# Running the last two units of an output product, and the first two of the next, token tile by token tile

## The chip, the cores and the metric

One core of a Trainium2 chip runs the whole kernel. The metric is the device time of that core in microseconds (us), and the time of a kernel is the median over its runs.

## The reference

A trunk of two layers works on 256 tokens of width 2048, in float32. Each layer is a token mixer, a cross attention into 256 fixed memory tokens (4 heads of 128), and an MLP with squared ReLU (2048 to 8192 and back). Layer 0's mixer is an mLSTM, layer 1's a gated DeltaNet with 32 value heads of 128 and a gate `z`. Every sub-layer is wrapped in two norms:

```python
for i in range(DEPTH):
    g = norm_g[i]
    h = rms_norm(x, g[0])
    mix = mlstm_mixer(h, ...) if i == 0 else gdn_mixer(h, ...)
    x = x + rms_norm(mix, g[1])
    h = rms_norm(x, g[2])
    x = x + rms_norm(mem_cross_attn(h, k_m, v_m, w_xq[i], w_xo[i]), g[3])
    h = rms_norm(x, g[4])
    x = x + rms_norm(sq_relu_mlp(h, w_up[i], w_down[i]), g[5])
```

and the end of the gated DeltaNet is `o = rms_norm(o, norm_g) * silu(z)`, then `o @ w_out`.

## The kernel before

**Precision and weights.** A float32 product is made of three matmuls on numbers split into a high part and a rest: high x high, high x rest, rest x high. Weights stream from memory in units of 4 blocks of 128 rows by 512 columns, each unit as two halves (`raw`, 512 KB each, 4 buffers). For each half ACT casts the high part (L89) and DVE subtracts to get the rest (L90); there are two buffers of each. `ws.add` lists the order of all units once; `ws.take` hands out the next one and starts the one after. `extra_unit` puts the first unit of the next product into tiles of the hidden units that are free by then (names `xw`, lines L85 and L86).

**Products.** `h` holds the sub-layer's input feature-major (features on the 128 partitions, the 256 tokens along the row, high part then rest), in 16 blocks of 128 features.
- `prod_feat` gives a feature-major result: weights are the stationary operand, 512 and 256 columns wide per step (L318, L319) or, narrow, three of 256 (L322 to L324). `fresh` makes the first four blocks narrow. `prod_tall` is the narrow form for one block of columns at a time (L337 to L339).
- `prod_tok` gives a token-major result (tokens on the partitions), in chunks of 512 columns: the input's token tile `t` (0 or 1, 128 tokens each) is stationary and 512 weight columns move (L384 to L386). For each unit it runs t=0, 12 matmuls, then t=1, 12 more.

**From one product to the next.** The output products m_out, xo, down and g_out are token-major, since the norm behind them is over a token's features. `Post.take` gets each chunk as it is done: sum of squares on ACT (`Rms.add`, L232), product with the norm's gain on DVE. With the last chunk (`ch == 3`) of a token tile it makes the reciprocal root `rpost` (`rstd`: L485 reduction, L487 or L489 and L490 root, L491 reciprocal). `advance` then adds the normed result to the residual stream `xk` (`residual`, L496, four chunks by two token tiles), transposes `xk` on PE (`feed`, L214, tiles `ltp`, eight transposes for each chunk), and splits the transposes into the new `h` (ACT L249, then DVE L250, 256 tokens wide). It also sums squares of the new `xk` for the next norm. `behind` fixes the order of some of these against each other. There are five such boundaries: m_out to xq, xo to up (layer 0), down to the gated DeltaNet's first product gq, g_out to xq, xo to up (layer 1). The last `down` has `stagger=True`: its last two units run t=0 of both, then t=1 of both, and each token tile goes to the output as it is done.

**Cross attention.** `xq` runs feature-major, narrow, for three heads, `ev_q` makes the scores and the softmax, and the fourth head's query is a `prod_tall` of its own.

**Gated DeltaNet.** The eight groups of four value heads run one after the other in `core`. A group loads `vt`, `tf`, `tn` and, last, `ab` (1.5 MB, single buffer, issued by the POOL queue), starts with small matmuls `np` (L1156) that need `ab`, and ends with `op` (L1218), the last reader of `ab`, and the transposes `otp` (L1241). Between the groups run the gate products `gz` (96 matmuls each, `gate(g4)`, groups 0 to 3, just ahead of the group's `core`) and, from group 4 on, the output product `g_out`. The gates of groups 4 to 7 are made earlier (`early_z`), kept in memory (`z_d`) and loaded by the POOL queue.

The order of instructions on each engine is fixed when the program is built: a scheduler places them by priority, and gives the DeltaNet's weight splits a higher one (`ws.first = 400`).

Of the kernel before, what the change touches and what calls it, by code (L numbers as in the profile page):

```python
# [14 lines left out]
P = 128  # L15
# [3 lines left out]
UK = 4  # L19
# [94 lines left out]
def trunk(ctx: ExitStack, tc, x, mem, norm_g, mem_norm_g, w_mem_kv, w_xq, w_xo, w_up, w_down,  # L114
# [22 lines left out]
    for l in range(2):  # L137
        if l == 1:
            g_in, g_out = gdn_w_in[0], gdn_w_out[0]
            for c in range(4):  # L140
                ws.add("gq", g_in, 0, D, c * 512, 512, tall=c > 0)
                ws.add("gk", g_in, 0, D, 2048 + c * 512, 512, tall=True)
                if c == 0:
                    ws.add("ab", g_in, 0, D, GDN_QKV + GDN_Z, 64, tall=True)
                ws.add("gz", g_in, 0, D, GDN_QKV + 2048 + c * 512, 512)
            ws.add("gv", g_in, 0, D, 4096, 4096, tall=True)
            ws.add("gz", g_in, 0, D, GDN_QKV, 2048)
            for half in range(2):
                ws.add("g_out", g_out, half * 2048, 2048, 0, D)
# [146 lines left out]
    def prod_feat(key, srcs, n_fb, evac, wide=True, before=None, fresh=False):  # L296


        nk = len(srcs)
        for c0 in range(0, n_fb, 4):  # L300
            nf = min(4, n_fb - c0)
            accs, k = None, 0
            while k < nk:
# [9 lines left out]
                w_ = wide and not (fresh and c0 == 0)  # L313
                for f, j in order:
                    a, kk = accs[f], k + j
                    wh, wl = hi[j][:, f * P : f * P + fw], lo[j][:, f * P : f * P + fw]
                    if w_:
# [8 lines left out]
            for f in range(nf):  # L326
                evac(c0 + f, Bank(accs[f], w_))
# [30 lines left out]
    def prod_tok(key, srcs, n_ch, evac, after=None, post=None, stagger=False, start=None):  # L358
# [3 lines left out]
        for c in range(n_ch):  # L362
            if start:
                start(c)
            accs = [acc(f"{key}{c}_{t}") for t in range(2)]
            k, units = 0, []
            while k < nk:
                final = post is not None and c == n_ch - 1 and k + UK >= nk
                if post is not None and (n_ch - c) * nk - k == 2 * UK:
                    extra_unit(4 if nk == UK else 0)  # L370
                hi, lo, kb, n = ws.take(key, 1 if final else None)
                if final:
                    post.halves = ws.begin()
                units.append((k, hi, lo, kb))
                k += kb
                if stagger and c == n_ch - 1 and k == nk - UK:
                    continue
                for t in range(2):
                    for k0, hi, lo, kb in units:
                        for j in range(kb):  # L380
                            kk = k0 + j
                            sh = srcs[kk][:, t * P : (t + 1) * P]
                            sl = srcs[kk][:, T + t * P : T + (t + 1) * P]
                            PE.matmul(accs[t], sh, hi[j], start=(kk == 0), stop=False)  # L384
                            PE.matmul(accs[t], sh, lo[j], start=False, stop=False)  # L385
                            PE.matmul(accs[t], sl, hi[j], start=False, stop=(kk == nk - 1))  # L386
                if after:
                    after(units[-1][0] // UK)
                units = []
            for t in range(2):  # L390
                evac(c, t, accs[t])
# [46 lines left out]
    class Post:  # L438


        def __init__(self, l, s, bias=None):
            self.l, self.s, self.bias, self.halves, self.g, self.r, self.late = l, s, bias, [], {}, [], []
            self.y = [acts.tile([P, 2, 512], F32, tag=f"y{c}", name=f"y{c}") for c in range(4)]
            self.rms = Rms("post")
# [12 lines left out]
        def take(self, ch, t, a, plus=False):  # L457

            d = self.y[ch][:, t, :]
            if plus:  # L460
                v = self.add(ch, t, a, False)
                a = d
            last = ch == 3 and t == 0 and self.halves
            if last:
                behind(self.rms.add(a, t, ch), self.halves.pop(0)()[0])
            else:
                self.rms.add(a, t, ch)
            if ch == 0 and t == 0:
                S.sqrt(warm, self.rms.ss[:, 0, 0:1])
            if ch == 3:  # L470
                self.r.append(self.rstd(t))
                late = lambda: V.tensor_tensor(d, a, self.g[ch], ALU.mult)
                if t == 0 and not plus:
                    late()
                else:
                    self.late.append(late)
                self.added = v if plus else None
# [5 lines left out]
        def rstd(self, t):  # L483
            r = small.tile([P, 1], F32, tag=f"rpost{t}", name="rpost")
            V.tensor_reduce(r, self.rms.ss[:, t, :], AX.X, ALU.add)  # L485
            if self.bias is None:
                S.activation(r, r, AF.Sqrt, bias=eps_t, scale=1.0 / D)  # L487
            else:
                V.scalar_tensor_tensor(r, r, 1.0 / D, self.bias[:, t : t + 1], ALU.mult, ALU.add)  # L489
                S.sqrt(r, r)  # L490
            V.reciprocal(r, r)  # L491
            return r

# [4 lines left out]
    def advance(post, nxt):  # L498

        rms = Rms("x")  # L500
        h = new_h()
        halves = post.halves
        r0 = post.residual(0, 0)
        if post.added:
            behind(r0, post.added)
        for ch in range(4):
            if ch:
                behind(post.residual(ch, 1), hv)
            else:
                hv = post.residual(0, 1)  # L510
            if ch < 3:
                behind(post.residual(ch + 1, 0), hv)
            ha, hv = feed(xk[ch], ch, h, lambda k: gain(nxt[0], nxt[1], k))
            if ch == 0:
                for late in post.late:
                    behind(late(), hv)
            for t in range(2):
                behind(rms.add(xk[ch][:, t, :], t, ch), ha)
            if ch < 2:
                for half in halves:  # L520
                    a, v = half()
                    behind(a, ha)
                    behind(v, hv)
                halves = ws.begin() if ch == 0 else []
        return h, rms
# [94 lines left out]
    def mlstm(sc, h, rms, before):  # L620
# [119 lines left out]
        return out_proj("m_out", y, 0, 1)  # L740

    def out_proj(key, y, l, s):
        post = Post(l, s)
        prod_tok(key, y, 4, post.take, post=post)
        return post


    def cross(sc, l, h, rms):
# [8 lines left out]
        def scales(c):  # L757
            if c == 3:
# [23 lines left out]
        prod_feat("xq", h, XA_H - 1, ev_q, wide=False, before=scales)  # L782
# [16 lines left out]
        return out_proj("xo", o, l, 3)  # L799
# [22 lines left out]
    def mlp(l, h, rms):  # L822
        post = Post(l, 5)
# [5 lines left out]
        post.bias = mlp_bias(rms)  # L829
        if l == 0:  # L830
            prod_tok("down", u, 4, lambda ch, t, a: post.take(ch, t, a, True), post=post)
            return post

        def last(ch, t, a):
            post.take(ch, t, a, True)
            if ch == 3:
                while post.late:
                    post.late.pop()()
# [5 lines left out]
        prod_tok("down", u, 4, last, stagger=True)  # L844
# [19 lines left out]
    def gdn(g0, h, rms):  # L864
# [8 lines left out]
        z_d = tc.dram_tile([4, P, 2, 512], F32, name="z_d")  # L873
# [36 lines left out]
        with tc.tile_pool(name="gd1", bufs=1) as sc:  # L910
# [126 lines left out]
            def early_z(c):  # L1037
# [6 lines left out]
                prod_tok("gz", h, 1, ev)  # L1044

            for c in range(4):
# [8 lines left out]
                early_z(c)  # L1055
# [64 lines left out]
        with tc.tile_pool(name="gd3", bufs=1) as sc:  # L1120
            post = Post(1, 1)
# [190 lines left out]
```

## Time and profile before

| | us |
|---|---|
| median of 3 runs | 2911.84 |
| the runs | 2912.97, 2911.84, 2908.85 |
| the profiled execution | 2910.57 |
| its span in the profile | 2908.8 |

The span is the time between the first and the last instruction that the profile records; 1.77 us of the execution's own time lie around it. Rows of the profile name an engine (PE is the matrix engine, PEld its load of the stationary operand, DVE the vector engine, ACT the scalar engine, POOL and SP mostly issue transfers), a line of the kernel (L214), the operation, the tiles that it writes and reads, and a count (x192). Of times, "busy" is the sum over instructions and "idle before" the time for which the engine waited, with what ended it. Matmuls are pipelined, so that their recorded lengths overlap. A window row gives the length of a stretch and for each engine the busy time and number of instructions in it, the granted clock of PE as a share of full speed (PEclk), the share of the transfer engines in use and GB/s.

### The profile page before, as it was taken

The page shows a single profiled execution, that of the slowest core. Times are in us where ns is not written, and L with a number is a line of the kernel's source. Part 1 is how long each engine was busy: PE and PEld are TensorE (multiplying, and loading weights), DVE is VectorE, ACT ScalarE, POOL GpSimd, SP SyncE. Part 2 cuts the span into 40 slices and gives each one's busy share as a digit, 9 for nine tenths or more (in the row PEclk, how much of TensorE's full clock was granted, in tenths as well). Part 3 has the DMA queues.
Part 4 walks back from the last instruction along what each step waited for, and adds up shares of the span by engine and source line. Part 5 has one row for each costly group of instructions (what it writes and reads, how often), then busy time and mean ns, then how long its engine had stood idle before and what let it go on. Part 6 is the DMA issues. An engine that isn't in the chain of part 4 may idle for free.

```text
span 2908.8 us, 42441 instructions
## 1 busy us (share of the span) xinstructions
PE 2866.5 (99%) x16683; PEld 2478.6 (85%) x16683; DVE 1756.9 (60%) x2603; ACT 1427.3 (49%) x2127; POOL 142.3 (5%) x295
## 2 busy tenths in 40 slices
PE   8999999999999999999999999999999999999998
PEld 7888888888888888799998997878888888888887
DVE  5554657654545555577776885554576545455565
ACT  6444546644434434467664545444465444344443
POOL 0000000000000000002212112220000000000000
PEclk9999999999999999999999999999999999999999
DMA  7545664555565555658778787664545555655555
GB/s 249 182 146 177 191 204 145 181 191 193 186 197 188 189 189 188 206 160 247 228 219 235 204 222 254 210 228 164 197 158 168 188 190 188 198 185 192 192 187 168
DMA packets 378411, 566.07 MB, mean 195 GB/s; under 512 B 23873, under 2 KB 156738, under 8 KB 375906
## 3 DMA queue, kind: packets, MB, share of 16 engines
q1 hardware_dynamic: 363456, 507.12, 56.0%
q0 software_dynamic: 13184, 54.90, 5.7%
q8 instruction: 131, 2.15, 0.3%
q10 hardware_dynamic: 1570, 1.33, 0.1%
q14 instruction: 70, 0.57, 0.1%
HBM read 535.94 MB, written 27.33 MB: 194 GB/s over the span
## 4 chain that ended last, share of the span: by engine, by line
PE 90%; DVE 4%; DMA 3%; ACT 1%; issue 1%; POOL 0%; DVEq 0%; ACTq 0%; POOLq 0%
PE up L318 15%; PE up L319 8%; PE down L384 8%; PE down L385 8%; PE down L386 8%; PE o L318 2%; PE g_out L386 2%; PE g_out L384 2%; PE g_out L385 2%; DMA raw<-in_gdn_w_in 2%; PE gz L384 2%; PE gz L386 2%; PE gz L385 2%; DVE lo L90 1%; PE gk L337 1%
## 5 line engine op out<-in xcount | busy, mean ns | idle before, releaser
L90 DVE TENSOR_TENSOR lo<-raw,hi 128x1024 fp32r<-128x1024 f32 x938 | 1110.2, 1217 | 895.1 <-ACT hi L89 894.1
L89 ACT CAST hi<-raw 128x1024 fp32r<-128x1024 f32 x938 | 943.4, 1046 | 944.7 <-PE down L386 314.3
L318 PE MATMUL up<-h,hi 128*128 128x512 f32 x1920 | 678.7, 399 | 0.0
L319 PE MATMUL up<-h,lo 128*128 128x256 f32 x1920 | 539.3, 281 | 0.0
L318 PEld LDWEIGHTS up<-h,hi 128*128 128x128 f32 x1920 | 360.8, 188 | 89.9
L385 PE MATMUL down<-lo,u 128*128 128x512 f32 x1024 | 398.5, 389 | 0.0
L384 PE MATMUL down<-hi,u 128*128 128x512 f32 x1024 | 398.4, 389 | 0.0
L386 PE MATMUL down<-hi,u 128*128 128x512 f32 x1024 | 398.3, 389 | 0.0
L319 PEld LDWEIGHTS up<-h,lo 128*128 128x128 f32 x1920 | 362.7, 189 | 0.2
L384 PEld LDWEIGHTS down<-hi,u 128*128 128x128 f32 x1024 | 192.2, 188 | 40.0
L386 PEld LDWEIGHTS down<-hi,u 128*128 128x128 f32 x1024 | 192.2, 188 | 40.0
L385 PEld LDWEIGHTS down<-lo,u 128*128 128x128 f32 x1024 | 192.2, 188 | 39.6
L337 PE MATMUL gv<-h,hi 128*128 128x256 f32 x512 | 147.1, 287 | 3.2 <-ACT hi L89 3.2
L339 PE MATMUL gv<-h,lo 128*128 128x256 f32 x512 | 146.6, 286 | 1.7 <-DVE lo L90 1.7
L338 PE MATMUL gv<-h,hi 128*128 128x256 f32 x512 | 145.9, 285 | 0.0
L384 PE MATMUL gz<-hi,h 128*128 128x512 f32 x256 | 103.7, 405 | 0.0
L337 PEld LDWEIGHTS gv<-h,hi 128*128 128x128 f32 x512 | 99.2, 194 | 3.8 <-ACT hi L89 3.4
L386 PE MATMUL gz<-hi,h 128*128 128x512 f32 x256 | 102.3, 400 | 0.0
L385 PE MATMUL gz<-lo,h 128*128 128x512 f32 x256 | 102.2, 399 | 0.0
L339 PEld LDWEIGHTS gv<-h,lo 128*128 128x128 f32 x512 | 99.2, 194 | 2.4 <-DVE lo L90 2.3
L338 PEld LDWEIGHTS gv<-h,hi 128*128 128x128 f32 x512 | 99.2, 194 | 0.2 <-issue 0.2
L889 DVE SCALAR_TENSOR_TENSOR cv<-pad,cols,cv 128x256 f32<-128x256 f32 x192 | 90.9, 480 | 6.3 <-ACT cv L887 3.8
(438 smaller groups left out, 4688.2 us busy)
## 6 DMA issues: line engine op xcount, KB each, us to landing
raw<-in_w_up SPq DMA_DIRECT2D x256, 512.0 KB, 4.0
raw<-in_w_down SPq DMA_DIRECT2D x256, 512.0 KB, 4.2
raw<-in_gdn_w_in SPq DMA_DIRECT2D x192, 512.0 KB, 5.0
raw<-in_mlstm_w_in SPq DMA_DIRECT2D x96, 512.0 KB, 3.9
raw<-in_gdn_w_out SPq DMA_DIRECT2D x64, 512.0 KB, 4.2
raw<-in_mlstm_w_out SPq DMA_DIRECT2D x32, 512.0 KB, 4.1
at_d<-at POOLq DMA_DIRECT2D x8, 1536.0 KB, 8.2
ab<-at_d POOLq DMA_DIRECT2D x8, 1536.0 KB, 6.9
```

The costliest lines, as they stand in the source:

```text
L89: a = nc.scalar.copy(h_, raw[:, :, :n])
L90: return a, nc.vector.tensor_tensor(l_, raw[:, :, :n], h_, ALU.subtract)
L318: PE.matmul(a[:fw], wh, srcs[kk][:, :], start=(kk == 0), stop=False, skip_group_check=True)
L319: PE.matmul(a[:fw, T:], wl, srcs[kk][:, 0:T], start=False, stop=(kk == nk - 1), skip_group_check=True)
L337: PE.matmul(a[:, 0:T], hi[k], srcs[k][:, 0:T], start=(k == 0), stop=False)
L338: PE.matmul(a[:, 0:T], hi[k], srcs[k][:, T:], start=False, stop=False)
L339: m = PE.matmul(a[:, 0:T], lo[k], srcs[k][:, 0:T], start=False, stop=(k == nk - 1))
L384: PE.matmul(accs[t], sh, hi[j], start=(kk == 0), stop=False)
L385: PE.matmul(accs[t], sh, lo[j], start=False, stop=False)
L386: PE.matmul(accs[t], sl, hi[j], start=False, stop=(kk == nk - 1))
L889: V.scalar_tensor_tensor(c, pad[:, j : j + T], w[j], c, ALU.mult, ALU.add)
```

## The change

1. `prod_tok` takes the last two units of a product that a `Post` follows together: t=0 of both, then t=1 of both (24 matmuls each). It does the same with the first two units of a product that has a `lead`.
2. `rpost` needs fewer steps at the end: `take` sums the first three chunks' squares and adds the bias ahead, with chunk 2 (`pre`). For t=0 the residuals of chunks 0 and 1 follow at once.
3. The transposes of a chunk go by token tile (`half`): four 128 x 128 transposes into one bank, then four 128-wide splits on ACT and four on DVE. For t=0, chunk 0's stand six matmuls before the end of the old product (`ahead`), chunk 1's right after it (`advance`); t=1's of chunks 0 and 1 stand between the parts of the next product's lead (`between`), and chunks 2 and 3 follow whole (`both`).
4. The next product begins token-major with its first two units: xq's three heads (384 wide, transposed back from `qtok`), the first 512 hidden units of `up` (transposed and split from `utok`). Ahead of gq stands a chunk of gz, the one that group 3's gate used to make in `gate(3)`; it is kept in `z_d` and group 3 now loads its gate as groups 4 to 7 do.
5. The last `down`'s `stagger` is now `split`, the same order.

```diff
+            ws.add("gz", g_in, 0, D, GDN_QKV + 1536, 512)
             for c in range(4):
...
-            ws.add("gz", g_in, 0, D, GDN_QKV, 2048)
+            ws.add("gz", g_in, 0, D, GDN_QKV, 1536)
...
+        pairs, i = [], 0
+        while i < len(steps):
+            two = i == 0 and lead or i == len(steps) - 2 and (post or split)
+            pairs.append((i, i + 1) if two else (i,))
+            i += len(pairs[-1])
+        for p_ in pairs:
+            last = p_[-1] == len(steps) - 1
+            if post and last:
+                extra_unit(4 if nk == UK else 0)
+            for i in p_:
+                fetch(i)
             for t in range(2):
-                evac(c, t, accs[t])
+                for i in p_:
+                    if t and i == p_[-1] and last and post:
+                        post.halves = ws.begin()
+                        run(i, t, 0, UK // 2)
+                        post.ahead()
+                        run(i, t, UK // 2)
+                    else:
+                        run(i, t)
+                    if lead and p_[0] == 0:
+                        lead.between(t * 2 + i)
+                    done(i, t)
...
+            if ch == 2:
+                p_ = self.pre[t] = small.tile([P, 1], F32, tag=f"pre{t}", name="pre")
+                V.tensor_reduce(p_, self.rms.ss[:, t, 0:3], AX.X, ALU.add)
+                V.scalar_tensor_tensor(p_, p_, 1.0 / D, self.bias[:, t : t + 1] if self.bias is not None else eps_t,
+                                       ALU.mult, ALU.add)
             if ch == 3:
-                self.r.append(self.rstd(t))
...
+                S.activation(r, self.rms.ss[:, t, 3:4], AF.Sqrt, bias=self.pre[t], scale=1.0 / D)
+                V.reciprocal(r, r)
+                if self.nxt and t == 0:
+                    self.residual(0, 0)
+                    self.residual(1, 0)
+                    self.late()
...
+        def half(self, ch, t):
+            p_ = psum(f"lth{ch}")
+            for i in range(4):
+                PE.transpose(p_[:, i * P : (i + 1) * P], xk[ch][:, t, i * P : (i + 1) * P], ident)
+            for i in range(4):
+                kb = ch * 4 + i
+                if t == 0:
+                    self.h[kb] = acts.tile([P, 2 * T], F32R, tag=f"h{kb}", name=f"h{kb}")
+                g_, d, s_ = gain(*self.nxt, kb), self.h[kb], p_[:, i * P : (i + 1) * P]
+                S.activation(d[:, t * P : (t + 1) * P], s_, AF.Copy, scale=g_)
+                V.scalar_tensor_tensor(d[:, T + t * P : T + (t + 1) * P], s_, g_, d[:, t * P : (t + 1) * P],
+                                       ALU.mult, ALU.subtract)
+        def both(self, ch):
+            for t in range(2):
+                self.residual(ch, t)
...
+            feed(xk[ch], ch, self.h, lambda k: gain(*self.nxt, k))
+        def ahead(self):
+            self.half(0, 0)
+            for half in self.halves:
+                half()
+        def advance(self):
+            self.half(1, 0)
...
+        def between(self, i):
+            if i == 0:
+                self.residual(0, 1)
+                self.half(0, 1)
+            elif i == 1:
+                self.residual(1, 1)
+                self.half(1, 1)
+                self.late()
+            elif i == 2:
+                self.both(2)
+            else:
+                self.both(3)
...
-        prod_feat("xq", h, XA_H - 1, ev_q, wide=False, before=scales)
+        prod_tok("xq", h, 1, lambda c, t, a: (V.tensor_copy, S.copy)[t](qtok[t], a), after=scales, lead=lead)
+        for f in range(XA_H - 1):
+            p_ = psum("xqt")
+            for t in range(2):
+                PE.transpose(p_[:, t * P : (t + 1) * P], qtok[t][:, f * P : (f + 1) * P], ident)
+            ev_q(f, Bank(p_, False))
...
+            if c == 0:
+                prod_tok("up", h, 1, first, lead=lead)
             u = new_u()
-            prod_feat("up", h, KB, relu2(u), fresh=c == 0)
+            if c == 0:
+                feed(d, 0, u, lambda k: None)
+            prod_feat("up", h, KB, relu2(u), f0=0 if c else 4)
...
+            early_z(0, lead)
...
-                early_z(c)
+                early_z(c + 1)
...
             def gate(g4):
                 zs = sc.tile([P, 2, 512], F32, tag="zs", bufs=2, name="zs")
+                if g4 > 2:
+                    nc.gpsimd.dma_start(zs, z_d[g4 - 3])
+                    return zs
```

More of the change, by code (lines that the diff above doesn't have):

```diff
@@ L294, in extra_unit, with prod_feat @@
             half()
-    def prod_feat(key, srcs, n_fb, evac, wide=True, before=None, fresh=False):
+    def prod_feat(key, srcs, n_fb, evac, wide=True, before=None, f0=0):
         nk = len(srcs)
-        for c0 in range(0, n_fb, 4):
+        for c0 in range(f0, n_fb, 4):
             nf = min(4, n_fb - c0)
@@ L356, in prod_few, with prod_tok @@
         return p_[:, 0 : 2 * n].rearrange("p (t n) -> p t n", t=2)
-    def prod_tok(key, srcs, n_ch, evac, after=None, post=None, stagger=False, start=None):
+    def prod_tok(key, srcs, n_ch, evac, after=None, post=None, start=None, lead=None, split=False):
         nk = len(srcs)
[L362 to L377, printed above, removed]
-                for t in range(2):
[L379 to L389, printed above, removed]
-            for t in range(2):
-                evac(c, t, accs[t])
@@ new lines, in prod_tok, with fetch, run @@
+        steps = [(c, k) for c in range(n_ch) for k in range(0, nk, UK)]
+        accs, units = {}, {}
+        def fetch(i):
+            c, k = steps[i]
+            if k == 0:
+                if start:
+                    start(c)
+                for t in range(2):
+                    accs[c, t] = acc(f"{key}{c}_{t}")
+            units[i] = ws.take(key, 1 if post and i == len(steps) - 1 else None)
+        def run(i, t, j0=0, j1=UK):
+            c, k = steps[i]
+            hi, lo, kb, n = units[i]
+            a = accs[c, t][:, :n]
+            for j in range(j0, j1):
+                kk = k + j
+                sh, sl = srcs[kk][:, t * P : (t + 1) * P], srcs[kk][:, T + t * P : T + (t + 1) * P]
+                PE.matmul(a, sh, hi[j][:, :n], start=(kk == 0), stop=False)
+                PE.matmul(a, sh, lo[j][:, :n], start=False, stop=False)
+                PE.matmul(a, sl, hi[j][:, :n], start=False, stop=(kk == nk - 1))
@@ new lines, in done @@
+        def done(i, t):
+            c, k = steps[i]
+            if k + UK == nk:
+                evac(c, t, accs[c, t][:, : units[i][3]])
+        pairs, i = [], 0
[9 more added lines that the diff above has]
+                fetch(i)
+            for t in range(2):
+                for i in p_:
[9 more added lines that the diff above has]
+                    done(i, t)
+            if after:
+                for i in p_:
+                    after(steps[i][1] // UK)
@@ L460, in take @@
             if plus:
-                v = self.add(ch, t, a, False)
+                self.add(ch, t, a, False)
                 a = d
[L463 to L467, printed above, removed]
+            self.rms.add(a, t, ch)
             if ch == 0 and t == 0:
                 S.sqrt(warm, self.rms.ss[:, 0, 0:1])
-            if ch == 3:
-                self.r.append(self.rstd(t))
[L472 to L477, printed above, removed]
+            if ch == 2:
[3 more added lines that the diff above has]
+                                       ALU.mult, ALU.add)
+            if ch == 3:
+                r = self.r[t] = small.tile([P, 1], F32, tag=f"rpost{t}", name="rpost")
+                S.activation(r, self.rms.ss[:, t, 3:4], AF.Sqrt, bias=self.pre[t], scale=1.0 / D)
+                V.reciprocal(r, r)
+                self.late = lambda: V.tensor_tensor(d, a, self.g[ch], ALU.mult)
+                if self.nxt and t == 0:
+                    self.residual(0, 0)
+                    self.residual(1, 0)
+                    self.late()
                 return
@@ L481, in take @@
                 self.load_gain(ch + 2)
[L483 to L492, printed above, removed]
         def residual(self, ch, t):
@@ L842, in last @@
                                                                 xk[i][:, t, :])
-        prod_tok("down", u, 4, last, stagger=True)
+        prod_tok("down", u, 4, last, split=True)
     def softplus(z, sc, n):
```

109 lines of the change are left out of this document (44 added, 65 removed).

## The prediction

> **What bounds the kernel now.** I read the page first (busy times, chain), then PE's waits, then windows around the places that the change touches.
>
> ```profile
> PE 2866.5 (99%) x16683; PEld 2478.6 (85%) x16683; DVE 1756.9 (60%) x2603; ACT 1427.3 (49%) x2127; POOL 142.3 (5%) x295
> PE 90%; DVE 4%; DMA 3%; ACT 1%; issue 1%; POOL 0%; DVEq 0%; ACTq 0%; POOLq 0%
> PE ltp L214 <- DVE xk L496: 10.9, 9, 1.8
> PE np L1156 <- DMA ab<-at_d: 2.3, 1, 2.3
> ```
>
> TensorE is busy for 99% of the span and carries 90% of the chain. What it lacks lies mostly at the boundaries, where the transposes `ltp` wait 10.9 us in nine places for the residual. There are five of them: B1 m_out to xq, B2 xo to up, B3 down to the gated DeltaNet, B4 g_out to xq, B5 xo to up. In each row below, a window from the end of the old product to the end of the next one's first stretch; then two places in B1 and B5.
>
> ```profile
> core 0: us, PE busy (x) PEld busy (x) DVE busy (x) ACT busy (x) POOL busy (x), PEclk, DMA share, GB/s
> 450.60:475.70 25.10, 23.25 (x178) 22.42 (x176) 19.44 (x37) 18.99 (x44) 0.00 (x0) 0.93 0.40 119
> 515.00:543.90 28.90, 27.20 (x224) 26.44 (x224) 23.57 (x43) 21.13 (x48) 0.00 (x0) 1.00 0.47 145
> 1231.30:1263.00 31.70, 29.05 (x227) 28.10 (x226) 23.28 (x42) 19.65 (x44) 0.00 (x0) 0.95 0.46 125
> 2116.30:2142.70 26.40, 23.28 (x178) 22.33 (x178) 21.78 (x39) 19.34 (x44) 0.00 (x0) 0.94 0.35 106
> 2180.90:2211.90 31.00, 28.63 (x224) 27.87 (x224) 24.36 (x46) 21.24 (x49) 0.00 (x0) 0.94 0.48 147
> ...
> 450.60:456.00 5.40, 3.55 (x21) 2.84 (x20) 3.58 (x9) 3.30 (x10) 0.00 (x0) 0.87 0.01 4
> ...
> 2185.10:2188.50 3.40, 3.40 (x17) 3.40 (x17) 3.25 (x7) 3.21 (x8) 0.00 (x0) 0.50 0.00 0
> ```
>
> DVE and ACT are busy for 19 to 24 us of each, 62 to 83%, and much of that is one chain: they can be the bound here. What the matmuls alone need follows from their pitch in undisturbed stretches:
>
> ```profile
> 1349.70:1372.70 23.00, 23.00 (x195) 23.00 (x193) 21.93 (x50) 20.82 (x28) 7.79 (x18) 1.00 0.97 302
> 640.00:680.00 40.00, 40.00 (x178) 33.12 (x177) 17.55 (x15) 17.51 (x20) 0.00 (x0) 1.00 0.60 196
> 448.05 0.60 ACT L232 ACTIVATE junk<-m_out 128x512 f32<-128x512 f32 x1 [1.23 <-PE m_out L386]
> 448.08 0.39 PE L385 MATMUL m_out<-lo,u 128*128 128x512 f32 x1
> 448.77 0.16 DVE L485 TENSOR_REDUCE rpost<-sspost 128x1 f32<-128x4 f32 x1 [0.96 <-ACT junk L232]
> 448.99 0.39 PE L386 MATMUL m_out<-hi,u 128*128 128x512 f32 x1
> 449.63 0.75 DVE L496 SCALAR_TENSOR_TENSOR xk<-y,rpost,xk 128x512 f32<-128x512 f32 x1
> 450.58 0.60 PE L214 MATMUL ltp<-ident,xk 128*128 128x128 f32 x4
> 453.02 1.10 PE L214 MATMUL ltp<-ident,xk 128*128 128x128 f32 x6 [1.84 <-DVE xk L496]
> ```
>
> A 256-wide matmul has 23.0/192, 0.120 us (a few records at its edges belong to neighbours); a 512-wide one (448.99−448.08)/4, 0.227 us; a transpose about 0.11. B1 needs 32 transposes and 144 narrow matmuls, 20.85 us, and takes 25.1: 4.25 too many. By the same sums B2 has 2.4 (26.65 of 29.05), B3 4.85, B4 5.6, B5 4.55 too many: 21.65 together, the ceiling of what the boundaries can give back. Part is waiting (in B1 1.84 us before 453.02, where the residual of the second token tile ends), part a clock at 0.50 for about 3.4 us after it (1.7 us), which B1, B3, B4 and B5 show and B2, with 1.7 us idle in pieces, doesn't.
>
> The Trainium skill (TensorE: Matmul & The Clock Gate, "Why this matters for your kernels") lets the clock fall only after PE gaps of over about 3 us; by that the four boundaries would have kept full clock and the ceiling would be 21.65 − 4 × 1.7 = 14.9. The trace disagrees, at 1.84 us.
>
> **Part 1: two units tile by tile, transposes by halves.** In before, t=1 of the last unit is 12 matmuls, 2.7 us, and the chain for t=0 (448.05 to 450.38, 2.33 us) just fits; t=1's own chain is bare. PE before at B1 (m_out ends, its next product is xq):
>
> ```order
> L384 MATMUL m_out_1_3698<-hi_3767,u_2418 128x512
> L385 MATMUL m_out_1_3698<-lo_3768,u_2418 128x512
> L386 MATMUL m_out_1_3698<-hi_3767,u_2418 128x512
> L214 MATMUL ltp_3887<-ident,xk_108 128x128 [waits DVE_49]
> L214 MATMUL ltp_3887<-ident,xk_108 128x128
> L214 MATMUL ltp_3888<-ident,xk_108 128x128 x2
> L214 MATMUL ltp_3887<-ident,xk_108 128x128 [waits DVE_49]
> ```
>
> PE now at the same place:
>
> ```order
> L519 MATMUL lth_3859<-ident,xk_108 128x128 [waits DVE_49]
> L519 MATMUL lth_3859<-ident,xk_108 128x128 x3
> L381 MATMUL m_out_1_3704<-hi_3773,u_2417 128x512
> L382 MATMUL m_out_1_3704<-lo_3774,u_2417 128x512
> L383 MATMUL m_out_1_3704<-hi_3773,u_2417 128x512
> L381 MATMUL m_out_1_3704<-hi_3773,u_2418 128x512
> L382 MATMUL m_out_1_3704<-lo_3774,u_2418 128x512
> L383 MATMUL m_out_1_3704<-hi_3773,u_2418 128x512
> L519 MATMUL lth_3891<-ident,xk_109 128x128 [waits DVE_49]
> L519 MATMUL lth_3891<-ident,xk_109 128x128 x3
> L381 MATMUL xq_0_3924<-xw_3783,h_3864 128x384 [waits Activation_49]
> ```
>
> Four t=0 transposes come six matmuls before the end, and t=0 of the new product bridges t=1's chain. But ACT must deliver its splits, and now stands like this there:
>
> ```order
> L525 ACTIVATE h_3864<-lth_3859,cols 128x128 [waits PE_49]
> L525 ACTIVATE h_3867<-lth_3859,cols 128x128 [waits DVE_49]
> L233 ACTIVATE junk,sspost<-m_out_1_3704 128x512 [waits PE_49]
> L525 ACTIVATE h_3896<-lth_3891,cols 128x128 [waits PE_49]
> L525 ACTIVATE h_3870<-lth_3859,cols 128x128 [waits DVE_49]
> L499 ACTIVATE rpost<-sspost,pre 128x1 [waits Activation_49]
> L89 CAST hi_3926<-raw_2_3930 128x2x384 [waits DMAHW3_49]
> L525 ACTIVATE h_3873<-lth_3859,cols 128x128 [waits DVE_49]
> ```
>
> A Square of t=1 and a weight cast have moved in among the first half's splits, each of which waits for DVE on its bank.
>
> ```profile
> L250 DVE SCALAR_TENSOR_TENSOR h<-ltp,cols,h 128x256 fp32r<-128x256 f32 x96 | 42.1, 478 | 8.3 <-ACT h L249 6.8
> L249 ACT ACTIVATE h<-ltp,cols 128x256 fp32r<-128x256 f32 x96 | 41.0, 472 | 25.6 <-PE ltp L214 17.4 <-DVE h L250 8.1
> L1234 DVE SCALAR_TENSOR_TENSOR zs<-op,ss,zs 128x128 f32<-128x128 f32 x64 | 17.8, 343 | 0.9
> L496 DVE SCALAR_TENSOR_TENSOR xk<-y,rpost,xk 128x512 f32<-128x512 f32 x48 | 34.2, 746 | 0.4
> L89 ACT CAST hi<-raw 128x1024 fp32r<-128x1024 f32 x926 | 933.7, 1049 | 938.9 <-PE down L386 314.3 <-PE up L318 189.1 <-issue 181.1
> ```
>
> A 128-wide split is not in the trace; between nothing saved (0.48) and half (0.24), I take 0.30, nearer the row of 343 less overlap. Each boundary trades 8 of 0.44 (the 42.1/96) for 16 of 0.30 on ACT and on DVE: 1.3 us more on each.
>
> Walk of B1, time 0 at t=1's first of 24 matmuls. Residuals of t=0 are ready from 2.4; transposes at 4.1; old product ends 5.9, second half's transposes 6.35. First half's splits, two engines in turn on one bank, 0.6 per block, with the Square (0.6+0.2) between: 4.5 to 7.7; second half's, after the cast (0.83 to 1.05), to about 11. t=1's residual comes at 8.3, its transposes and splits share the engines, and the two later quarters (residuals 4 × 0.7, eight splits of 0.44) end near 19; the last 24 of 96 matmuls and what piled up behind them end at 28.3. Six transposes of the token-major query add 0.65. From 5.45: 23.5, **1.6 less** than 25.1. (A 384-wide matmul is not in the trace; bounds 0.120 and 0.227, I take 0.17: 16.3 for 96.) By the Trainium skill (TensorE: Matmul & The Clock Gate, "Wait — 56ns, not 53.3ns?") it would take N/2.4 + 2.5 ns, an estimate of 0.162, and the two xq boundaries 0.7 us less each.
>
> The other walks differ by their queues. B4, like B1 with the add: 24.5 for 26.45, **−1.95**. B5 (96 512-wide for 192 narrow, 21.8 for 23.1, plus eight transposes for the hidden units, 0.9): 30.0 for 31.2, **−1.2**. B2 the same, but there was no half clock to remove, and a cast of 1.05 stands between the first half's splits: 30.2 for 29.05, **+1.15**. B3: four casts and the priority of the DeltaNet's weights stand ahead of the splits; 4.8 too many for 4.85, **0**. Boundaries: **−3.6**. Bounds: −21.65 (all gone), and +6.3 (two more casts, 1.05 each, ahead of the first splits at three of them).
>
> Smaller: the query goes through a copy, transposes and a copy before attention, 1.3 us later, of which 48 narrow matmuls (5.8 us) cover part: +0.5 each layer, **+1.0** (0 to 2.6). The last unit is wanted 12 matmuls, 2.7 us, sooner: **+0.7** (0 to 3). At the end, the reduction and the bias leave the chain before the output:
>
> ```profile
> 2901.22 0.16 DVE L485 TENSOR_REDUCE rpost<-sspost 128x1 f32<-128x4 f32 x1 [0.79 <-ACT junk L232]
> ...
> 2901.89 0.15 DVE L489 SCALAR_TENSOR_TENSOR rpost<-rpost,s 128x1 f32<-128x1 f32 x1
> 2902.07 0.20 ACT L490 ACTIVATE rpost<-rpost 128x1 f32<-128x1 f32 x1 [0.89 <-DVE rpost L489]
> ```
>
> **−0.4**: the ACT step can start 0.4 us after 2901.22 and not 0.85.
>
> **Part 2: a gz chunk moves from group 3 of g_out to the front.** Its 96 matmuls cost the same there. But in the group stage they were cover: `np` of the next group needs `ab`, whose load starts after the last `op` that reads the single buffer. Windows from the last `op` to the next `np`:
>
> ```profile
> 1866.70:1880.70 14.00, 14.00 (x66) 11.20 (x64) 9.69 (x19) 9.55 (x13) 1.63 (x3) 1.00 0.84 278
> ...
> 1952.80:1962.20 9.40, 7.06 (x36) 5.23 (x35) 6.96 (x17) 5.62 (x10) 1.63 (x3) 1.00 0.96 358
> 1962.20:1966.00 3.80, 3.80 (x40) 3.06 (x41) 1.27 (x4) 0.00 (x0) 0.00 (x0) 0.64 0.80 287
> ...
> ab<-at_d POOLq DMA_DIRECT2D x8, 1536.0 KB, 6.9
> ```
>
> PE before, from group 2's last `op` (first rows; 58 matmuls in all follow, which are the 14.0 us):
>
> ```order
> L1218 MATMUL op<-vt,ab 128x128 x6
> L386 MATMUL gz_1_17124<-hi_17125,h_10293 128x512
> L384 MATMUL gz_1_17124<-hi_17125,h_10294 128x512
> L385 MATMUL gz_1_17124<-lo_17126,h_10294 128x512
> L386 MATMUL gz_1_17124<-hi_17125,h_10294 128x512
> ```
>
> and now, nine g_out matmuls, the last three of them:
>
> ```order
> L381 MATMUL g_out_1_17522<-hi_17523,u_16293 128x512
> L382 MATMUL g_out_1_17522<-lo_17524,u_16293 128x512
> L383 MATMUL g_out_1_17522<-hi_17523,u_16293 128x512
> L1299 MATMUL otp<-ident,zs 128x128 [waits DVE_49]
> L1299 MATMUL otp<-ident,zs 128x128 [waits DVE_49,Activation_49]
> ```
>
> 58 fillers are now 9, with eight `otp`: 9 × 0.227 + 0.9, 2.9 us, against 6.9 to 7.0: **4.1 us idle**. After group 3 about 21 follow its last `op`: 21 × 0.227 + 0.9 = 5.7, **1.3 idle**. Three later ones have 27, 7.0 us, no idle at 6.9; one such waited 2.3 before (1952.80): **−0.5** on a mean. And after 4.1 us of idle, the clock of 0.50 for 3.4 us, as in B5, **+1.5**: in before, the 2.3 us at 1962.20 were followed by the clock of 0.64 in the row above. In all **+6.4** (0 if loads land in under 3 us; 15 if they land at 8).
>
> The sum: 2910.57 (span 2908.8 and 1.77 around it) − 3.6 + 1.0 + 0.7 − 0.4 + 6.4 (4.1 + 1.3 − 0.5 + 1.5) = **2914.7**. The profiled run is 1.3 under the median 2911.84, so this is +0.1% on the median, within 0.2% (5.8 us, about what a measurement of this kernel can tell from none).
>
> **Rivals.** (a) The half transposes do cover the chain: PE never pauses for over a few tenths and the clock stays full at all boundaries. For it: the waits are short (1.84 the longest), and half of each next product's first quarters is now free of t=1. Against: the order of ACT above, and 16 splits for 8. It gives two thirds of 21.65, −14.4, for −3.6: 2904. It decides if the boundaries give over 12. (b) `ab` lands late at every transition. Landing at 8.0 instead of 6.9, as half-way to the 9.4 of 1952.80, idle is 5.1, 2.3 and three times 1.0, 10.4, and each of the five brings a half clock of 1.7, 8.5; less the 2.3 + 1.7 of before, +14.9 in place of 6.4: 2923. For it: the queues are at 0.96 share there. Against: 6.9 is the median of eight. It decides from a landing of about 7.4, where all five wait and bring their half clock. (c) The cover was not needed, as the scheduler could run other work there: +0, 2908. Against: the row order above.
>
> **Numbers.** Forecast 0.50 (2910 to 2918), (a) 0.20, (b) 0.22, (c) 0.08. Range 2901 to 2924: it reaches a little past (a) and (b), and leaves out their outer parts, some 4 tenths of each, 0.17. Chances: faster (under 2906) 0.20, all (a); same (2906 to 2917.6) 0.52, forecast and (c) less the forecast's upper edge 0.06; slower 0.28, (b) and that edge.
>
> **What would show it.** Right: PE waits for `ab` twice, about 4 and 1 us, with a clock of 0.50 after; `lth` waits vanish, but matmuls of xq, up and gz wait for the splits of `h`, and boundaries are within 2 us of before. Wrong: windows of 2 to 3 us less at each boundary (a), or no wait of `np` at group 3 (c).

## The result

| | before | changed |
|---|---|---|
| median, us | 2911.84 (7 runs, 2908.77 to 2917.09) | 2919.26 (7 runs, 2915.17 to 2926.2) |
| profiled execution, us | 2910.57 | 2915.17 |
| its span, us | 2908.8 | 2913.5 |

The changed kernel takes 1.0028 times as long as the one before, 95% interval 1.0018 to 1.0038. Its profiled execution is the lowest of its seven. The page of the changed kernel (busy times, chain), then some rows of what PE waited for:

```profile
PE 2872.3 (99%) x16423; PEld 2463.2 (85%) x16423; DVE 1762.3 (60%) x2649; ACT 1430.7 (49%) x2163; POOL 144.4 (5%) x298
PE 91%; DVE 3%; DMA 2%; ACT 2%; issue 1%; POOL 0%; DVEq 0%; ACTq 0%; POOLq 0%
...
PE otp L1299 <- DVE zs L1292: 3.6, 2, 2.8
PE gq L338 <- DVE lo L90: 2.1, 2, 1.2
PE gv L336 <- ACT hi L89: 2.1, 1, 2.1
PE up L381 <- ACT h L525: 1.8, 6, 0.7
PE xp L1229 <- ACT v L962: 1.4, 1, 1.4
PE gz L381 <- ACT h L525: 1.1, 1, 1.1
PE xq L381 <- ACT h L525: 0.7, 2, 0.4
```

The 10.9 us for which the transposes waited for the residual are gone; 1.8, 1.1 and 0.7 us of waits of up, gz and xq for ACT's part of the splits of `h` have come (and 0.8 us each of up and gz for DVE's part), and 3.6 us in the group stage of the DeltaNet. The five boundaries follow, each from the end of the old product (less 0.4 us and a little more, for the four transposes that now stand inside it) to the end of the lead, which no longer ends where before's rows end:

```profile
core 0: us, PE busy (x) PEld busy (x) DVE busy (x) ACT busy (x) POOL busy (x), PEclk, DMA share, GB/s
449.60:472.00 22.40, 21.82 (x128) 19.47 (x127) 18.93 (x41) 19.41 (x51) 0.00 (x0) 1.00 0.50 145
511.60:542.00 30.40, 28.96 (x129) 21.65 (x128) 23.64 (x48) 21.09 (x52) 0.00 (x0) 0.94 0.49 149
1230.40:1259.60 29.20, 27.19 (x131) 21.34 (x130) 21.42 (x42) 21.90 (x52) 0.55 (x1) 1.00 0.45 139
2122.40:2146.60 24.20, 22.91 (x128) 19.65 (x127) 20.31 (x44) 19.50 (x51) 0.00 (x0) 1.00 0.45 134
2187.90:2216.30 28.40, 27.02 (x127) 20.76 (x126) 21.65 (x43) 19.96 (x51) 0.00 (x0) 1.00 0.48 145
```

PE is idle for 0.6, 1.4, 2.0, 1.3 and 1.4 us in them. Only B2 runs at half clock in this trace, the one that didn't before; in after_again it is B5 instead. Where the time went is read from the start of the same instruction in both traces: each row gives what a stretch takes longer than in before (the 96 matmuls of the moved chunk, 21.8 us, and the four transposes that stand in an old product, 0.44, are set off where they moved). B1 is counted from the last two units of m_out on, the others from the end of the old product; B1 and B4 end at the first scores `xs`. Two further traces of the changed kernel, after_again and after_3, stand beside it.

| us more than before | predicted | first trace | after_again | after_3 |
|---|---|---|---|---|
| up to m_out | 0 | −1.4 | 0.0 | −0.7 |
| B1, B2, B3, B4, B5 | −1.6, +1.15, 0, −1.95, −1.2 | −0.8, +2.3, −1.4, −0.7, −1.8 | −1.0, +0.4, −1.5, −0.7, −1.7 | −0.6, +2.3, −1.4, −0.7, −3.1 |
| boundaries in all | −3.6 | −2.4 | −4.4 | −3.4 |
| queries and xo, both layers | +1.7 | +0.2 | +1.7 | +0.1 |
| DeltaNet: gk to the start of gv | 0 | +4.3 | +3.8 | +4.1 |
| gv | 0 | −2.5 | −2.3 | +2.2 |
| group stage to the end of g_out | +6.4 | +7.1 | +7.9 | +6.2 |
| behind the last matmul | −0.4 | −0.5 | −0.5 | −0.5 |

At the first `xs` the changed kernel has already run 9 (B1) and 10 (B4) of the fourth head's 48 query matmuls, about 1.1 us each time, which before runs behind it. So B1 and B4 gave about 1.1 us more each than their rows say, and the queries cost 2.2 us more; the total is not touched.

### The profile page after: what moved, and what is told of

Its sections match the earlier page's. It is cut to its first block, busy times and chain, and to the rows that moved or that the text cites. A ratio compares the mean times of both kernels' runs of the same rounds, so it can differ in the third digit from the quotient of the medians.

```text
span 2913.5 us, 41994 instructions
## 1 busy us (share of the span) xinstructions
PE 2872.3 (99%) x16423; PEld 2463.2 (85%) x16423; DVE 1762.3 (60%) x2649; ACT 1430.7 (49%) x2163; POOL 144.4 (5%) x298
## 4 chain that ended last, share of the span: by engine, by line
PE 91%; DVE 3%; DMA 2%; ACT 2%; issue 1%; POOL 0%; DVEq 0%; ACTq 0%; POOLq 0%
PE up L317 15%; PE down L381 8%; PE down L382 8%; PE down L383 8%; PE up L318 8%; PE o L317 2%; PE g_out L381 2%; PE g_out L383 2%; PE g_out L382 2%; PE gv L338 2%; PE gv L336 2%; PE gv L337 2%; PE gz L381 1%; PE gz L383 1%; DVE lo L90 1%; PE gz L382 1%
## 5 line engine op out<-in xcount | busy, mean ns | idle before, releaser
L381 PE MATMUL gz<-hi,h 128*128 128x512 f32 x248 | 100.3, 405 | 0.0
L383 PE MATMUL gz<-hi,h 128*128 128x512 f32 x248 | 98.9, 399 | 0.0
```

Of the source, the lines that this page charges most:

```text
L381: PE.matmul(a, sh, hi[j][:, :n], start=(kk == 0), stop=False)
L383: PE.matmul(a, sl, hi[j][:, :n], start=False, stop=(kk == nk - 1))
```

## The experiments

Theory 1 at this point: the boundaries give back what the sum says, some 3 us, and the moved chunk of gz costs 6 to 8, since PE stands idle where it was cover. Its rival, theory 2: the moved chunk is neutral, and the loss comes from the boundaries.

**lead_early: the lead without the moved cover.** Another chunk of gz, the first that was made early anyway, is the lead; group 3 makes its own gate again.

```diff
-            ws.add("gz", g_in, 0, D, GDN_QKV + 1536, 512)
+            ws.add("gz", g_in, 0, D, GDN_QKV + 2048, 512)
...
-                early_z(c + 1)
+                if c:
+                    early_z(c)
...
-                if g4 > 2:
-                    nc.gpsimd.dma_start(zs, z_d[g4 - 3])
+                if g4 > 3:
+                    nc.gpsimd.dma_start(zs, z_d[g4 - 4])
```

> The changed kernel with another chunk of gz as the token-major lead: the first of the four gates that were made early anyway. Group 3 makes its own gate again, 58 matmuls stand between group 2's last op and group 3's np, as before the change; between the pairs of groups 0 and 1 no gz stands any more. Theory 1 (the loss sits in the group stage, where the moved chunk was cover): from group 3 to the end of g_out about 6 us less than in the changed kernel, 0 to 4 us more at the pairs of groups 0 and 1; time 2 to 6 us under the changed kernel, ratio to the kernel before 0.999 to 1.002. Theory 2 (the loss comes from the boundaries, and the moved chunk is neutral): no difference to the changed kernel beyond 1 us, ratio 1.003.

Measured: 1.0001 times before, interval 0.9992 to 1.0010; median 2911.0 us, where the changed kernel, measured beside it, had 2917.6. The stretch from group 2's last `op` to group 3's `np` in its trace, and its one wait there:

```profile
1866.00:1880.10 14.10, 14.10 (x68) 11.29 (x69) 9.70 (x19) 9.64 (x13) 1.63 (x3) 1.00 0.81 282
...
PE np L1216 <- DMA ab<-at_d: 2.1, 1, 2.1
```

The fillers are back, PE is not idle, and the group stage takes 0.3 us more than before instead of 7.1. The boundaries are much as in the changed kernel: from the end of the old product's last matmul to that of the lead's last, B1, B2, B4 and B5 take 21.9, 29.9, 23.5 and 28.0 us there and 21.9, 30.0, 23.6 and 27.9 here; B3 takes 28.7 and, with a half clock, 29.6. Theory 2 falls.

**gz_moved: the moved chunk alone.** The kernel before, with only the chunk moved (made after the whole `h`):

```diff
+            ws.add("gz", g_in, 0, D, GDN_QKV + 1536, 512)
...
+            early_z(0)
             for c in range(4):
...
+                if g4 > 2:
+                    nc.gpsimd.dma_start(zs, z_d[g4 - 3])
+                    return zs
```

> The kernel before with only the chunk of gz moved from group 3 to the front (the whole h is made first, as before; no pairs, no half transposes). Theory 1: the group stage loses 5 to 7 us as in the changed kernel, the boundary into the DeltaNet is 0 to 1 us different, so the kernel is 4 to 8 us slower than before, ratio 1.0015 to 1.003. Theory 2: the time of before within 1.5 us, ratio 0.9995 to 1.0005.

Measured: 1.0031 times before, 1.0019 to 1.0043; median 2919.4 us, 9.2 more than before, a little past the 4 to 8 expected. This is the whole loss of the change, with none of its boundaries. Its trace shows the same idle time, ended by the same products `zs`:

```profile
PE otp L1243 <- DVE zs L1236: 3.6, 2, 2.8
...
1892.80:1900.50 7.70, 4.05 (x18) 2.85 (x16) 5.48 (x13) 4.55 (x6) 1.10 (x2) 0.79 0.73 275
1897.30:1904.10 6.80, 5.23 (x45) 4.37 (x46) 5.15 (x13) 1.81 (x4) 0.53 (x1) 0.50 0.93 351
```

3.65 of the 7.7 us are idle, and 6.8 us at half clock follow, in which PE is busy for 5.2 us and so loses 2.6. Its group stage takes 4.4 us more than before, where the changed kernel takes 7.1, and the stretch from gk to gv 3.4 us more, as in the changed kernel. The boundary into the DeltaNet, with twice the half clock of before, takes 1.6 us more.

**What PE waits for there.** The prediction said `ab`. The trace of the changed kernel says something else (timeline after group 2's last `op`, with the rows of other instructions left out, then a window):

```profile
1889.43 0.56 POOL L1203 DMA_DIRECT2D ab<-at_d  x1 [1.45 <-PE op L1276]
1889.78 1.28 ACT L1287 ACT_TABLE_LOAD   x1
1891.32 0.20 DVE L1288 RECIPROCAL ss<-ss 128x8 f32<-128x8 f32 x1 [0.64 <-ACT ss L1287]
1891.64 0.87 DVE L1292 SCALAR_TENSOR_TENSOR zs<-op,ss,zs 128x128 f32<-128x128 f32 x3
1892.04 0.33 PE L1299 MATMUL otp<-ident,zs 128*128 128x128 f32 x1 [0.84 <-DVE zs L1292]
1892.42 2.35 DVE L90 TENSOR_TENSOR lo<-raw,hi 128x1024 fp32r<-128x1024 f32 x2
1894.69 1.38 DVE L1292 SCALAR_TENSOR_TENSOR zs<-op,ss,zs 128x128 f32<-128x128 f32 x5
1895.18 1.59 PE L1299 MATMUL otp<-ident,zs 128*128 128x128 f32 x7 [2.81 <-DVE zs L1292]
1896.70 0.53 PE L1214 MATMUL np<-tn,ab 32*32 32x32 f32 x12
...
1895.60:1902.40 6.80, 6.80 (x52) 4.48 (x51) 3.15 (x8) 1.79 (x4) 0.53 (x1) 0.50 0.81 286
```

The transposes `otp` stand ahead of `np` on PE. They wait for the products `zs`, between whose third and fourth DVE subtracts two weight halves, 2.35 us. (Ahead of the square root, ACT loads a table for 1.28 us; DVE's part of the chain is done 0.4 us before that ends.) `ab` was issued at 1889.43 and landed at 1896.27 by the trace, and `np` starts at 1896.70: two paths that end within half a us of each other. Three kernels take one or the other away.

**ab_halves: `ab` earlier.** Of the changed kernel; `np` needs the first half alone, which is free after `cp`.

```diff
+            ab = g0.tile([P, 6, 4, P], F32, tag="at", name="ab")
             def core(grp, zs, ys):
...
-                ab = g0.tile([P, 6, 4, P], F32, tag="at", name="ab")
-                nc.gpsimd.dma_start(ab, at_d[grp])
                 aa, aq = ab[:, 0:3], ab[:, 3:6]
+                nc.gpsimd.dma_start(aa, at_d[grp, :, 0:3])
+                nc.gpsimd.dma_start(aq, at_d[grp, :, 3:6])
```

> The changed kernel with the load of ab in two parts, of which np needs only the first, whose last reader is cp and not op: it can start some 3 us earlier and has half the bytes. Theory 1a (as predicted: np waits for ab): the idle time between group 2's last op and group 3's np, 4 us, goes, and the half clock with it; 4 to 7 us less than the changed kernel. Theory 1b (the chain op, square, root, zs, otp ends last, as the releaser DVE zs of the changed kernel's trace says, and ab only just behind it): otp still waits about 3.6 us for zs there, at most 0.5 us is gained, the half clock stays.

Measured: 1.0045 times before, 1.0029 to 1.0061, no gain at all. The wait there, and the stretch:

```profile
PE otp L1301 <- DVE zs L1294: 3.6, 2, 2.8
...
1889.00:1896.70 7.70, 4.05 (x18) 2.86 (x16) 5.48 (x13) 4.56 (x6) 1.10 (x2) 0.88 0.90 303
...
ab<-at_d POOLq DMA_DIRECT2D x16, 768.0 KB, 4.9
```

The halves land in 4.9 us, and still the idle 3.65 us stay: the stretch takes 7.7 us here and in gz_moved, 7.6 in the changed kernel's first trace. Theory 1b holds: the chain to `zs` ends last.

**zs_first and zs_only: the chain shorter, with `ab` in halves and whole.** `zs` gets a higher priority than the weight splits, so that its eight products stand together:

```diff
+                        with tc.high_priority(offset=2000):
-                        V.scalar_tensor_tensor(zs[:, tt, s_], ops[tt][:, s_], ss[:, tt, hh : hh + 1], zs[:, tt, s_],
-                                               ALU.mult, ALU.mult)
+                            V.scalar_tensor_tensor(zs[:, tt, s_], ops[tt][:, s_], ss[:, tt, hh : hh + 1], zs[:, tt, s_],
+                                                   ALU.mult, ALU.mult)
```

> The kernel ab_halves with the eight products zs ahead of the weight subtractions on DVE, at a higher priority; the scheduler then also moves 10 to 13 fillers of the later groups from behind op to behind np. If the idle 3.6 us after group 2 had two causes in parallel (the chain to zs, which the two subtractions of 2.35 us lengthen, and ab): with both gone the wait of otp falls to about 1 us and the half clock of 6.8 us goes, 4 to 6 us less than the changed kernel. If the fillers alone matter: the later groups, now with 18, wait too, and it is no faster than the changed kernel.

> The same as zs_first with ab loaded whole, as in the changed kernel. If ab is the second cause: np waits for ab in place of otp for zs after group 2, the sum stays at about 4 us, and after groups 3 and 5 to 7, where 18 fillers and 8 transposes (5.0 us) stand against a landing of 6.9 us, np waits about 1.9 us each: 4 to 12 us slower than the changed kernel. If ab lands in time: as zs_first.

Measured: 1.0022 (1.0010 to 1.0034) and 1.0023 (1.0010 to 1.0036). The same stretch in zs_first, then in zs_only, each with what PE waited for:

```profile
1893.90:1899.80 5.90, 4.50 (x20) 2.86 (x18) 4.50 (x13) 4.44 (x6) 1.10 (x2) 0.98 0.81 277
PE gv L336 <- ACT hi L89: 7.5, 1, 7.5
PE otp L1302 <- DVE zs L1295: 0.6, 1, 0.6
PE g_out L381 <- ACT u L250: 0.8, 1, 0.8
```

```profile
1898.00:1904.80 6.80, 5.02 (x22) 3.14 (x21) 5.37 (x13) 4.93 (x7) 1.63 (x3) 1.00 0.78 280
PE np L1214 <- DMA ab<-at_d: 0.9, 3, 0.4
PE otp L1300 <- DVE zs L1293: 0.6, 1, 0.6
PE g_out L381 <- ACT u L250: 0.8, 1, 0.8
```

With `ab` alone taken away the stretch stays 7.7; with the subtractions alone, 6.8, and `np` now waits 0.4 us there for `ab`; with both, 5.9. So the stretch has two causes in parallel, and the nearer one was not the one predicted. The comparison is not quite clean: the scheduler also put 12 (zs_first) and 14 fillers (zs_only) there in place of 9, some of them between the transposes, where 0.8 us is a new wait of g_out for the group's own result `u`. The size in zs_only was missed: it kept 26 fillers at the later groups, where zs_first has 17 at three of four, and there `np` waited 0.4 us at most. The 4 to 6 us that zs_first was to gain over the changed kernel don't show in its time: 1.0022 stands against 1.0028 and 1.0033, with overlapping intervals. Both traces also have the wait of gv that is the subject further down, 7.5 and 7.0 us for 2.1 in the first trace of the changed kernel, so that their total times say little about the group stage.

**before_halves and early_halves: `ab` in halves where 26 fillers stand.** The same edit on the kernel before, and on lead_early, whose waits for `ab` are 2.3 and 2.1 us at group 6.

> The kernel before with the load of ab in two parts and nothing else. Its one wait of np for ab (2.3 us) and the half clock behind it (1.7 us) go if ab alone binds there: 2 to 4 us less, ratio 0.9985 to 0.9995. If zs binds with it: no difference, ratio 0.9997 to 1.0003.

> The kernel lead_early with the load of ab in two parts, the first free after cp. lead_early's trace has one wait of np for ab, 2.1 us, and no half clock in the group stage. If ab is what binds where 26 fillers stand: that wait goes, 1.5 to 3 us less than lead_early, 2908 or so, ratio to before 0.999 to 1.000. If the chain to zs binds there too: another wait of about 2 us, on otp, takes its place, and the time stays.

Measured: before_halves 0.9987 times before, 0.9977 to 0.9996 (median 2906.4 us), faster than both kernels; early_halves 0.9993, 0.9981 to 1.0004. In before_halves the stretch ahead of group 6's `np`, 9.4 us in before with 2.3 idle, shows no wait:

```profile
1951.66:1957.57 5.91, 5.89 (x30) 4.26 (x29) 4.00 (x13) 2.69 (x6) 1.63 (x3) 1.00 0.92 314
```

The scheduler also put 21 fillers there instead of 26. Where the chain to `zs` is covered, `ab` is what binds. The changed boundaries add nothing that can be measured in the time: lead_early stands to before as 1.0001, early_halves and before_halves are 0.9993 and 0.9987 with overlapping intervals. In lead_early's trace the stretch from gk to gv, with its own chunk of gz moved out of it, takes 2.0 us more than in before and the queries and xo 1.7, which is about what the boundaries give (3 us).

**after_again, after_3, ab_halves_2, ab_halves_3, before_2: what varies.** The times of the changed kernel spread over 17 us, those of ab_halves lay at 2920 to 2930 in five of six, its profiled one at 2913.7.

> The changed kernel once more, to see which of its stages vary from execution to execution: its profiled execution was the lowest of seven (2915.2, median 2919.3). If the spread is the clock, the busy matmul count and the waits stay and only the stretches at 0.50 differ in number and length (27 us of them in the first profile, each us costs half a us); if it is transfers, the waits for raw weights or ab differ.

> The kernel ab_halves once more, to have a trace of an execution of its upper level: five of its six took 2920 to 2930 us, the profiled one 2913.7. If the clock makes the difference, the matmuls and waits are those of the first trace, and some 20 us more stand at 0.50 in one stage, 10 us longer; the place tells whether it is behind the idle 3.6 us after group 2. If not, a wait of several us shows that the first trace hasn't.

> The same again: one of the two should be of the upper level (five in six).

> The changed kernel a third time: five of its 15 times lie above 2921 us. If this one does, the same place and the same number of us at 0.50 as in ab_halves is expected; if not, the stretches of the first two traces (1328, 1769, 1895).

> The kernel before once more, for a second trace. The changed order shows a wait of 6.4 to 7.7 us of gv for a weight half near the end of gv in five of nine traces (2.1 to 3.2 us in the other four); the four traces with the chunk in group 3 show 1.8 to 3.2 us. If the long wait belongs to the moved chunk, this one has 2 to 3 us again and a span of 2902 to 2912 us; if it is chance in the transfers whatever the order, it can show 6 to 8 us here too, and a span of 2913 or more.

Measured: after_again 1.0033 (1.0019 to 1.0048), after_3 2918.7, ab_halves_2 2923.5, ab_halves_3 2928.0 and before_2 2909.3 us in single runs. The group stage shows the same 3.6 us in all four of the first. What differs is a wait near the end of gv for a weight half, and the clock behind it (below the waits in after_3, ab_halves_3 and before_2; in ab_halves_3 two stretches of clock 0.50 as well):

```profile
PE gv L336 <- ACT hi L89: 7.3, 1, 7.3
```

```profile
PE gv L336 <- ACT hi L89: 6.4, 1, 6.4
...
1775.30:1785.50 10.20, 5.93 (x26) 5.64 (x27) 6.39 (x9) 5.11 (x7) 0.00 (x0) 0.50 0.72 259
1819.70:1829.90 10.20, 10.20 (x52) 8.08 (x51) 1.61 (x3) 3.22 (x5) 2.37 (x4) 0.50 0.31 110
```

```profile
PE gv L337 <- ACT hi L89: 2.0, 1, 2.0
```

So it isn't the clock alone, as the first alternative had it: the cast ahead of that matmul waits 11.5 us in after_3, for its weights by the trace, where it waits 6.3 and 7.4 us in the first traces of the changed kernel and of before. Behind it the clock stays at 0.50 for 10.2 us in after_3, ab_halves_2 and ab_halves_3, and for 6.8 in zs_first and zs_only. The two halves are issued while the DeltaNet's own tables (`t_d`, `tn_d`, `v_d`, `ab`) move; the order of issue around them is the same in before, in the changed kernel and in ab_halves but for the halves of `ab`. The long wait (6.4 to 7.7 us) stands in five of the nine traces with the chunk moved, and in none of five with it in place (1.8 to 3.2 us). Five long waits spread by chance over these 14 traces would miss all five of the second kind in about one case of 16, so the counts speak for the move, but they don't show it: nothing in the order there explains it, and no run took it away by itself.

## Why the prediction was right or wrong

**The sum.** +4.1 us was forecast, 2914.7 for the profiled execution, which took 2915.17. That this fits to 0.5 us is luck: the execution is the lowest of its seven, and in it a term that the sum put at nothing (+4.3 from gk to gv) meets others that came out lower (−2.5 in gv, −1.4 ahead of B1, 0.2 instead of 1.7 for the queries). By the medians +7.4 us came: in the range, but past 2917.6, below which the likeliest case, "same", was to stay. What came is "slower", by the moved chunk as forecast, at a chance of 0.28. (The prediction's lengths of B2, B4 and B5 lie up to 0.2 us beside its rows, 28.90, 26.40 and 31.00; nothing hangs on that.)

**Part 1, right in sum.** −3.6 was forecast for the boundaries, −2.4, −4.4 and −3.4 were measured. The reason held too: the wait for the residual goes (10.9 us), but each chunk's 128-wide splits on two engines take its place. PE's idle time shows only part of that: in B4 the lead's first 20 matmuls take 4.7 us from first to last start, where the pitch below would give 3.3, and only 0.4 us of it is recorded as idle. The splits took 0.32 and 0.34 us where 0.30 was estimated (rows of the changed kernel):

```profile
L525 ACT ACTIVATE h<-lth,cols 128x128 fp32r<-128x128 f32 x80 | 27.0, 370 | 5.3 <-DVE h L526 3.7 <-PE lth L519 1.5
L526 DVE SCALAR_TENSOR_TENSOR h<-lth,cols,h 128x128 fp32r<-128x128 f32 x80 | 25.7, 345 | 3.3 <-ACT h L525 2.9
464.10:471.90 7.80, 7.80 (x47) 7.68 (x45) 6.31 (x9) 5.86 (x10) 0.00 (x0) 1.00 0.47 144
```

The last row has the 384-wide matmuls undisturbed: 45 in 7.8 us, 0.173 each. 0.17 was taken; the estimate of 0.162, worked out by the Trainium skill (TensorE: Matmul & The Clock Gate, "Wait — 56ns, not 53.3ns?"), is too low for this stream. Single boundaries were off by up to 1.5 us: B3, for which 0 was forecast, lost its half clock (−1.4 to −1.5), and B2 cost 2.3 us instead of 1.15 in the two traces in which it got one, 0.4 in the third. B4's row says −0.7 for −1.95, but with the fourth head's 1.1 us added it gave 1.8, and B1 with its own 1.1 about 2.

**Smaller terms.** The queries and the earlier last unit cost 0.1 to 1.7 us for +1.7 by the table, and 2.2 more when the fourth head's matmuls are counted with them. The end gained 0.5 for 0.4: the root L499 follows the accumulation on ACT at once.

```profile
2906.19 0.19 ACT L233 ACTIVATION_READ_ACCUMULATOR junk<-y 128x1 f32 x1
2906.41 0.29 ACT L499 ACTIVATE rpost<-sspost,pre 128x1 f32<-128x1 f32 x1
2907.02 0.16 DVE L500 RECIPROCAL rpost<-rpost 128x1 f32<-128x1 f32 x1
```

**Part 2, right in size, wrong in the wait.** +6.4 was forecast for the group stage, 6.2 to 7.9 came, and with the chunk back (lead_early) 0.3. The step "4.1 us idle, since `np` waits for `ab`" failed in its cause: 3.65 us of waiting are `otp`'s for `zs`, and in none of the three traces does `np` wait for `ab` there; its load ends just ahead of that chain, and an earlier load changes nothing (ab_halves). The prediction counted the eight `otp` as fillers, though each of them waits for the chain of squares, root and products that begins at `op`. Behind group 3, where 1.3 idle were forecast, there is 0.8 in three pieces, none of them for `ab` (7.5 us from `op` to `np` in all): 21 fillers covered nearly all of it.

The terms fit less well than their sum. The half clock lasted 6.8 us, 3.4 lost, not 1.5; and before's wait of 2.3 us at group 6 went in full, with the half clock behind it (1.7 us), where only −0.5 was set down. Added up, 3.65 + 0.8 + 3.4 − 2.3 − 1.7 is 3.8 of the 7.1 us of the first trace; with 2.6 lost at half clock it is 3.0 of the 4.4 of gz_moved. In the changed kernel 1.4 us more are a wait of `xp` for `v` at the start of the stage, which lead_early has too (2.2) and gz_moved hasn't, so that it doesn't come with the chunk. Where the remaining 1.4 (gz_moved) to 2 us arise is open.

**What the sum lacked.** The stretch from gk to gv takes 3.8 to 4.3 us longer in the three traces, and 3.4 in gz_moved; the forecast put it at nothing. Two things in it are new: 10.2 us at clock 0.50 in the changed kernel, where before has 6.8 (1.7 us), and 2.1 us of waits of gq for weight subtractions, for which before's waits have no row. The two windows, changed and before:

```profile
1329.00:1339.20 10.20, 10.20 (x31) 8.06 (x30) 1.93 (x6) 4.00 (x5) 3.03 (x4) 0.50 0.36 105
```

```profile
1311.30:1318.10 6.80, 6.80 (x21) 5.66 (x22) 1.64 (x6) 2.06 (x4) 3.02 (x4) 0.50 0.59 154
```

Part of it is what varies anyway: the four other traces with group 3's chunk in place take 0.3 to 2.2 us more than before's first trace in this stretch, two of them with the same 10.2 us of half clock; the nine with it moved take 2.5 to 5.6. So some of it comes with the chunk, by a way that no run shows. With the long wait in gv in some executions, some 5 us each, this is the likely difference between the forecast and the median.

**The rivals.** (a) did not come: idle time at the boundaries fell from 11.7 to 6.7 us, and of before's four half clocks none is left, with a new one at B2, but the longer chain of splits and the query's detour took most of it back. (b) did not come either: three transitions with 27 fillers show no wait over 0.2 us, and the loads landed in 6.8. (c) fell with gz_moved.

## What to carry to other kernels

Work that looks movable may be, as here, the cover for a wait elsewhere: count what stands between the last reader of a buffer and the first user of its next load, and what else in between waits for the same point, before taking it away. Instructions that themselves hang on the chain are no filler for it. A boundary whose wait is short is worth little, if the cure adds instructions to the engines that already make the chain.

## What the runs showed of the hardware

PE's clock fell to 0.50 after short idle times, and not after every one of them. In zs_first 1.4 us in two pieces ahead of 1899.6 were followed by 3.4 us at 0.50, in B2 of the changed kernel 1.3 us in four pieces, while zs_only with 1.8 us in three pieces after group 2 and B3 with 2.0 kept the full clock. Near 1329 in the changed kernel 10.2 us at 0.50 follow on only 0.3 us of idle time in 10 us; the last matmuls ahead of it there are 26 small ones, 16 of them with two columns. So the idle sum alone doesn't decide it, and the rule of about 3 us that the Trainium skill gives (TensorE: Matmul & The Clock Gate, "Why this matters for your kernels") is too generous for this kernel. Apart from those at the very end of a trace, a low stretch lasts 3.4, 6.8 or 10.2 us in these traces, and costs half of the time for which PE is busy in it.
